# A two-layer decoder trunk: recurrence outputs normed four heads at a time, row norms taken per token, one block row's transfers on GpSimd

## The chip, the cores and the metric

The kernel runs on one core of a Trainium2 chip. The core has a matrix engine (PE, with its weight loads listed as PEld), a vector engine (DVE), a scalar engine with lookup tables (ACT), a general engine (POOL, also called GpSimd) and a queue engine (SP, also called SyncE). Each runs its own list of instructions in order; they meet at semaphores. DMA transfers are issued by SP and by POOL here. The metric is the time of one execution in microseconds (us).

## The reference, cut to what matters

Everything is float32, with 256 tokens of width 2048. Layer 0 mixes by two head groups side by side, spatial gating (A) and a gated linear recurrence (B), layer 1 by attention with a forget gate (C). Each is followed by a gated MLP with a short convolution. Every block starts with a row norm over the 2048 channels of a token.

```python
def rms_norm(x, gain):
    y = x * rsqrt(mean(x * x, axis=-1) + 1e-6); return y * gain

u, v, q, f, i, g = split(rms_norm(x) @ w_in)       # layer 0: six parts of 1024 columns
v = rms_norm(gelu(v) per head); y_a = gelu(u) * (causal(w_s) @ v + b)
k, decay = (1 - lb) * sigmoid(-f), lb + (1 - lb) * sigmoid(f)      # 8 heads of 128
o[t] = sum over s <= t of (q[t] . k[s], decayed from s to t) * i[s]
y_b = rms_norm(o per head) * silu(g)               # the norm that the change regroups
x = x + concat(y_a, y_b) @ w_out

q, k, v, g, f = split(rms_norm(x) @ w_c)           # layer 1: f has one column per head, 16
c = cumsum(log_sigmoid(f + b_f))                   # along the tokens
s = q @ k.T / sqrt(128) + c[t] - c[s]; y = softmax(causal s) @ v * sigmoid(g)
x = x + y @ w_out
```

The row factor rsqrt(mean(x*x)+eps) of a token is called R below. It multiplies a whole row, so the kernel may apply it to the products instead of to x. The norm of a recurrence head over its 128 channels has the same form; a factor R that multiplied q of token t multiplies all of o[t].

## The kernel before, in words

**Weights.** 820 pieces of 512 KB (some smaller) come from HBM through SP, into four buffers. `weights` (L179 to L183) issues the load; `halves` rounds the piece on ACT to the form that the profile calls fp32r (`wh`, L175) and subtracts on DVE what was lost (`wl`, L176). Each of the two has three buffers. The activations are split in the same way, and PE adds three products, high by high, high by low and low by high (L311 to L313 in `project_four`, L292 to L294 in `project_tok`, L266 and L269 in `project`). A weights piece feeds a dozen 128x512 matmuls in most projections.

**All other work goes between the pieces.** It is written as generators. `tick()` (L127) is called ahead of each weights piece and advances each generator in flight by one yield; `depth` says how many may be in flight and the rest wait in `queue`. `held(r)` and `tied(r)` order an instruction of a generator behind the newest weights operation or matmul, without a semaphore. Within these orders a scheduler at build time lists each engine's instructions by its own costs.

**Transposition of block rows.** `blocks` (L323) transposes 32x32 squares on DVE into `tmp`; `moves` (L327 to L333) sends 16 transfers of 32 KB to turn the squares' order, eight from SP and eight from GpSimd in alternation (L331).

**Layer 0, `mixer_ab` (L486).** The row norm of x sums squares into `acc` (128 channels-in-a-tile by 256 tokens). `Norm.finish` (L443 to L452) multiplies a matrix of ones by `acc` (L445), which gives the row sums along the free dimension on all 128 partitions, and makes R, 128x256; `finish_tok` (L430) makes the same factors with tokens on partitions, Rt, 128x2, from four small matmuls (L434). A matmul with a reversing matrix (L594) turns the second column of Rt upside down for the values of the recurrence (Rr).

The recurrence is a generator per head, `hgrn(h)` (L667 to L755). It takes three times a PSUM bank of the two of the pool `px`: `dg` for the diagonal (16 small matmuls, L681), `xps` for the levels (L714 to L721), `op` for the output (L743 to L745). The output of a head, 128 by 256, is squared and summed on ACT straight from the bank, once for each half of the tokens (L749), the factor is made (L751, a logarithm and an exponential on ACT), and two scaled copies take the output out of the bank to `o` (L753). For q, `fold` (L335 to L339) adds the two halves of the product and L802 and L803 multiply by R. `gated` (L768) multiplies the output by silu of the gate and sends the result through `blocks` and `moves`. Ahead of the projection the pieces of `w_g` and `w_u` go by, four heads each.

The output projection reads `w_abo` (L847 to L860), a quarter q of the output channels at a time. `add_four` (L460) evicts a quarter, transposes it with `blocks` and `moves` (all 16 at once for q = 0 and 3, in two lots for q = 1 and 2), and later adds it to x (L474) and feeds the next norm. The first four pieces of the second quarter are multiplied ahead of the last two of the first.

**Layer 1, `mixer_c` (L866).** `norm.finish()` (L888) makes R again, since the forget gate has tokens along the free dimension. `forget` (L896 to L902) multiplies the 16 gate columns by x in four 32-partition groups; `sums` (L904 to L929) adds the groups, multiplies by R (L919), takes log-sigmoid and the running sum (L926), and writes it to HBM (L928). `spread` (L931 to L934) reads it back to all partitions, four heads at a time, in 512 KB; `attend` adds it to the scores (L958).

The code that the profile's lines belong to:

Of the kernel before, what the change touches and what calls it, by code (L numbers as in the profile page):

```python
# [8 lines left out]
F32 = mybir.dt.float32  # L9
# [10 lines left out]
NH = 8  # L20
# [33 lines left out]
def tile_trunk(ctx: ExitStack, tc: tile.TileContext, x, pp_d, cst_d, mlev_d, msk_d,  # L54
# [12 lines left out]
    def nm(base):  # L67
        count[0] += 1
        return f"{base}_{count[0]}"
# [44 lines left out]
    def bank():  # L114
        return psum["pool"].tile([P, 512], F32, tag="px", name=nm("px"), bufs=psum["banks"])
# [211 lines left out]
    def moves(tmp, dst, queues=(nc.sync, nc.gpsimd), rows=range(4)):  # L327
        n = 2 * BLK
        for a in rows:
            for b in range(4):  # L330
                queues[(a + b) % len(queues)].dma_start(dst[BLK * b:BLK * (b + 1), :, a * n:(a + 1) * n],  # L331
                                  tmp[BLK * a:BLK * (a + 1), b * 4 * n:(b + 1) * 4 * n]
                                  .rearrange("p (m r) -> p m r", m=4))  # L333

    def fold(ps):  # L335
        t = tp.tile([P, S], F32, tag="ev", name=nm("ev"), bufs=3)
        SC.activation(t, ps[:, S:2 * S], AF.Copy)
        V.tensor_tensor(t, ps[:, 0:S], t, ALU.add)
        return t  # L339

    def project_norm(wsrc, acts, R, out=None, run=2):
        t = fold(project(wsrc, acts, run=run))
        if out is None:
            out = t
        V.tensor_tensor(out, t, R, ALU.mult)
        return out

    def split(dst, src, gain=None, eng=SC, turn=False):
        if turn:
            h, lo = (dst[:, i * S:(i + 1) * S].rearrange("p (t n) -> p t n", t=2) for i in range(2))  # L350
# [49 lines left out]
    class Norm:  # L400
# [39 lines left out]
            rsq(Rt, p2[:, 0:4].rearrange("p (t two) -> p t two", two=2)[:, :, 0], D)  # L440
            self.Rt = Rt

        def finish(self, tok=False):  # L443
            ps = bank()
            PE.matmul(ps[:, 0:S], ones, self.acc, start=True, stop=True)  # L445
            R = cp.tile([P, S], F32, tag="R", name=nm("R"), bufs=2)
            rsq(R, ps[:, 0:S], D)
            if not tok:
                return R
            for _ in self.finish_tok():  # L450
                pass
            return R, self.Rt  # L452
# [7 lines left out]
    def add_four(q, ps, z, tmp, dst, nxt, halves=1):  # L460
        for T in range(2):
            SC.activation(z[:, T], ps[T], AF.Copy)
        blocks(lambda T: z[:, T], tmp)
        moves(tmp, dst, rows=range(4 // halves))

        def rest():
            if halves == 2:
                yield
                moves(tmp, dst, rows=range(2, 4))
            for _ in range(LAG - 2 * (q == 3)):  # L470
                yield
            for i in range(4):
                m = 4 * q + i
                held(V.tensor_tensor(xT[m], xT[m], dst[:, i], ALU.add), "wl")  # L474
                nxt.feed(m)
                if q < 3 or i % 2:
                    yield
            if q == 3:
                for _ in range(WAIT):
                    yield  # L480
                yield from nxt.finish_tok()

        queue.append(rest())


    def mixer_ab(norm):  # L486
# [8 lines left out]
            return hp.tile([P, S], F32, tag="mg" if n == "mg" else "lf", name=nm(n), bufs=NH)  # L495


        gv, late = [], []

        def finish():  # L500
            for k in range(KT):
                norm.feed_square(k)
                if k % 2:
                    yield
            late.extend(norm.finish(tok=True))

        for g, ps in enumerate(project_first(w_v, norm, lambda: queue.append(finish()))):
            v = hp.tile([P, 2, 512], F32, tag="tok", name=nm("gv"), bufs=2)
            gv.append(v)
            if g == 0:  # L510
                SC.activation(v[:, 0], ps[0], AF.Copy)
                SC.activation(v[:, 1], ps[1], AF.Copy)
            else:
                drain()
                R, Rt = late
                last = ps
        A = norm.a

# [71 lines left out]
                yield  # L590


        ps = bank()
        PE.matmul(ps[:, 0:2], cst[:, K_REV:K_REV + P], Rt, start=True, stop=True)  # L594
        Rr = hp.tile([P, LANE], F32, tag="Rr", name="Rr")[:, 0:2]
        V.tensor_copy(Rr[:, 0:1], Rt[:, 0:1])
        V.tensor_copy(Rr[:, 1:2], ps[:, 1:2])


        gam = pp[:, C_GAM:C_GAM + 3 * NH]  # L600
# [6 lines left out]
        def bound():  # L607
# [9 lines left out]
            V.tensor_tensor(lb, e3[0], sm_, ALU.mult)  # L617
            V.tensor_scalar(lb, lb, 2.0 ** -63, None, ALU.max)

        queue.append(mixes())  # L620
        lf, kq = [], []

# [28 lines left out]
        depth[0] = 5  # L651

        itoks, left, os_ = [], [NH], []


        H = P // 2
# [10 lines left out]
        def hgrn(h):  # L667
# [75 lines left out]
            tied(PE.matmul(op[:, 0:P], st[:, 0], i0, start=True, stop=True))  # L743
            tied(PE.matmul(op[:, P:S], s128, i0, start=True, stop=False))
            tied(PE.matmul(op[:, P:S], s1, i1, start=False, stop=True))  # L745
            so = hp.tile([P, LANE], F32, tag="so", name=nm("so"), bufs=2)[:, 0:2]
            ot = hp.tile([P, P], F32, tag="ot", name=nm("ot"), bufs=1)
            for T in range(2):
                SC.activation(ot, op[:, T * P:(T + 1) * P], AF.Square,  # L749
                              accum_out=so[:, T:T + 1])  # L750
            rsq(so, so, P)  # L751
            for T in range(2):
                SC.activation(os_[h // 4][:, T, d0:d0 + P], op[:, T * P:(T + 1) * P], AF.Copy,  # L753
                              scale=so[:, T:T + 1])
            left[0] -= 1  # L755

        gz = []
# [36 lines left out]
        for h in range(NH):  # L794
            if h in (4, 7):
                values(len(itoks))
            while len(kq) <= h:
                tick()
            if h % 4 == 0:
                os_.append(hp.tile([P, 2, 512], F32, tag="o", name=nm("o"), bufs=2))  # L800
            z = fold(project(w_q[h], A))
            V.tensor_tensor(kq[h][:, 2], z[:, 0:P], R[:, 0:P], ALU.mult)  # L802
            V.tensor_tensor(back(kq[h][:, 1]), z[:, P:S], R[:, P:S], ALU.mult)  # L803
            queue.append(hgrn(h))
        for j in range(2):
            ps = project_four(w_g[4 * j:4 * j + 4], A, KT)
# [38 lines left out]
        for q in range(4):  # L845
            if q == 0:

                ps = stretch(0, (0, 2, 4, 6, 8, 10), more=True)
                ahead = stretch(1, (0, 2, 4, 6), more=True)
                stretch(0, (12, 14), ps=ps)  # L850
            elif q == 1:
                ps = stretch(1, (8, 10, 12, 14), ps=ahead)
            else:
                ps = stretch(q, range(0, KT, 2))
            z = hp.tile([P, 2, 512], F32, tag="tok", name=nm("zo"), bufs=2)
            tmp = hp.tile([P, 1024], F32, tag="E", name=nm("tmp"), bufs=2)
            dst = wide("dst").rearrange("p (m t) -> p m t", m=4)
            if q == 0:
                depth[0] = 2
            add_four(q, ps, z, tmp, dst, nxt, 2 if q in (1, 2) else 1)  # L860
        es.close()
        banks(ctx, 4)
        return nxt
# [2 lines left out]
    def mixer_c(norm):  # L866
# [18 lines left out]
        early.append(project_tok(w_cqkv[CH // 4], norm))  # L885
        drain()
        depth[0] = 2
        R, Rt = norm.finish(), norm.Rt  # L888
        yB = []
        gq = hp.tile([P, LANE], F32, tag="gq", name="gq")[:, 0:1]  # L890
        V.tensor_scalar(gq, pp[:, C_QN:C_QN + 1], float(P) ** -0.5, None, ALU.mult)
# [4 lines left out]
        def forget():  # L896

            ps = pm.tile([P, 512], F32, tag="pm", name=nm("pm"))
            for k in range(KT):
                r = k % 4 * BLK  # L900
                PE.matmul(ps[r:r + CH, 0:S], w2[:, k], xT[k], start=k < 4, stop=k >= KT - 4, skip_group_check=True)
            return ps  # L902

        def sums(ps, fc):  # L904
            yield
            yield
            f, fa, on = (hp.tile([CH, S], F32, tag=n, name=n) for n in ("f", "fa", "on"))
            c = hp.tile([P, 512], F32, tag="f2", name="f2")[0:CH].rearrange("p (g n) -> p g n", g=2)
            for g, t in ((1, c[:, 0]), (2, c[:, 1]), (3, f)):
                r = SC.activation(t, ps[BLK * g:BLK * g + CH, 0:S], AF.Copy)  # L910
                if g == 1:
                    held(r)
            yield
            held(V.tensor_tensor(f, ps[0:CH, 0:S], f, ALU.add), "wl")
            for g in range(2):
                V.tensor_tensor(f, f, c[:, g], ALU.add)
            V.memset(fc, 0.0)
            V.memset(on, 1.0)
            V.tensor_tensor(f, f, R[0:CH], ALU.mult)  # L919
            V.tensor_scalar(f, f, pp[0:CH, C_BF:C_BF + 1], None, ALU.add)  # L920
            yield
            held(SC.activation(fa, f, AF.Abs))
            act(fa, fa, AF.Exp, scale=-1.0)
            act(fa, fa, AF.Ln, bias=one1[0:CH])
            V.scalar_tensor_tensor(f, f, 0.0, fa, ALU.min, ALU.subtract)
            V.tensor_tensor_scan(fc[0:CH], on, f, 0.0, ALU.mult, ALU.add)  # L926
# [73 lines left out]
        for g in range(CH // 4):  # L1000
            qkv = []
            ss = hp.tile([P, 2, 2, LANE // 4], F32, tag="ss", name=nm("ss"), bufs=2)[..., 0:4]
            for j in range(3):
                if g == 0 and j == 2:
                    fc, cd = hp.tile([P, S], F32, tag="fc", name="fc"), []
                    queue.append(sums(forget(), fc))
# [294 lines left out]
```

## Time and profile before

| | |
|---|---|
| runs | 2288.38, 2287.43 and 2288.41 us, median 2288.38 |
| span of the profiled execution | 2287.3 us (the page gives no other time for it) |
| instructions | 32261, of them 10832 matmuls |
| granted PE clock | full in all 40 slices |
| HBM read | 435.24 MB; DMA mean 210 GB/s |
| busy | PE 2280.8, DVE 1559.8, ACT 1309.6, POOL 361.2 us |

The profile is one execution; its span is 1.1 us below the median of the three runs. In a row of the timeline the columns are start, duration, engine, line, operation, output and inputs, sizes and count; a bracket at the end gives the engine's idle time before it and what ended it. Matmuls overlap, so the distance of two starts tells more than a duration. A group row gives busy time and mean nanoseconds of one, then the idle time before the group.

### The profile page before, as it was taken

The numbers are of one execution on the slowest core, as the hardware profiler recorded it, in microseconds if no ns is written. First come the engines' busy times: TensorE is split into PE (matmuls) and PEld (weight loads), VectorE is DVE, ScalarE is ACT, GpSimd is POOL, SyncE is SP. The second block draws the span as 40 slices with busy tenths as digits, with TensorE's granted clock in tenths as the row PEclk, the third lists the DMA queues.
The fourth block names the chain that finished last, engine by engine and source line by source line (L and its number), as shares of the span: only waits on it lengthen the run. The fifth ranks groups of instructions, "written<-read, shape, count | busy, mean of one in ns | idle before, by whom it ended". The sixth has DMA issues, their size and how long they took to land.

```text
span 2287.3 us, 32261 instructions
## 1 busy us (share of the span) xinstructions
PE 2280.8 (100%) x10832; PEld 1893.5 (83%) x10832; DVE 1559.8 (68%) x2309; ACT 1309.6 (57%) x1980; POOL 361.2 (16%) x662
## 2 busy tenths in 40 slices
PE   9999999999999999999999999999999999999999
PEld 8888888888888888888888888888888888888887
DVE  7788767777467656766875675767776476657766
ACT  7677756666456445654565555655665465456642
POOL 0121221212012002111111111211211012012102
PEclk9999999999999999999999999999999999999999
DMA  8655767778667667776666655777777677667765
GB/s 288 195 169 160 215 199 235 238 216 234 193 208 221 206 201 213 220 213 186 213 227 203 194 177 181 220 224 242 225 217 218 195 216 210 209 205 216 223 204 174
DMA packets 489415, 480.45 MB, mean 210 GB/s; under 512 B 114112, under 2 KB 457168, under 8 KB 489120
## 3 DMA queue, kind: packets, MB, share of 16 engines
q1 hardware_dynamic: 467040, 453.54, 64.2%
q0 software_dynamic: 20480, 22.50, 4.3%
q10 hardware_dynamic: 1728, 2.35, 0.3%
q8 instruction: 85, 1.39, 0.3%
q14 instruction: 82, 0.67, 0.1%
HBM read 435.24 MB, written 2.11 MB: 191 GB/s over the span
## 4 chain that ended last, share of the span: by engine, by line
PE 97%; DVE 2%; ACT 1%; issue 0%; SPq 0%; DMA 0%; DVEq 0%; ACTq 0%
PE pm L311 26%; PE pm L312 26%; PE pm L313 26%; PE pm L292 4%; PE pm L294 4%; PE pm L293 4%; PE pm L193 1%; PE pm L266 1%; PE pm L217 1%; DVE wl L176 0%; PE pm L269 0%; ACT wh L175 0%; DVE kq L701 0%; PE px L955 0%; SPq L331 0%
## 5 line engine op out<-in xcount | busy, mean ns | idle before, releaser
L176 DVE TENSOR_TENSOR wl<-w,wh 128x1024 fp32r<-128x1024 f32 (+1 forms) x820 | 996.9, 1219 | 637.0 <-ACT wh L175 629.3
L175 ACT ACTIVATE wh<-w 128x1024 fp32r<-128x1024 f32 (+1 forms) x820 | 862.5, 1054 | 786.0 <-PE pm L313 552.3
L311 PE MATMUL pm<-wh,a 128*128 128x512 f32 x1728 | 674.4, 390 | 0.0
L312 PE MATMUL pm<-wl,a 128*128 128x512 f32 x1728 | 672.5, 389 | 0.0
L313 PE MATMUL pm<-wh,a 128*128 128x512 f32 x1728 | 672.5, 389 | 0.0
L331 POOL DMA_DIRECT2D zt<-tmp x413 | 223.5, 549 | 1201.6 <-DVE tmp L324 1089.8
L313 PEld LDWEIGHTS pm<-wh,a 128*128 128x128 f32 x1728 | 324.4, 188 | 67.4
L312 PEld LDWEIGHTS pm<-wl,a 128*128 128x128 f32 x1728 | 324.4, 188 | 67.3 <-DVE wl L176 0.5
L311 PEld LDWEIGHTS pm<-wh,a 128*128 128x128 f32 x1728 | 324.4, 188 | 67.1
L311 PE MATMUL pm<-wh,hid 128*128 128x512 f32 x688 | 267.6, 389 | 0.0
L312 PE MATMUL pm<-wl,hid 128*128 128x512 f32 x688 | 267.6, 389 | 0.0
L313 PE MATMUL pm<-wh,hid 128*128 128x512 f32 x688 | 267.6, 389 | 0.0
L331 POOL DMA_DIRECT2D turn<-tmp x160 | 86.7, 550 | 504.5 <-DVE tmp L324 256.7
L292 PE MATMUL pm<-wh,a 128*128 128x512 f32 x416 | 165.2, 397 | 0.0
L294 PE MATMUL pm<-wh,a 128*128 128x512 f32 x416 | 162.1, 390 | 0.0
L293 PE MATMUL pm<-wl,a 128*128 128x512 f32 x416 | 162.0, 389 | 0.0
L311 PEld LDWEIGHTS pm<-wh,hid 128*128 128x128 f32 x688 | 129.2, 188 | 26.9
L313 PEld LDWEIGHTS pm<-wh,hid 128*128 128x128 f32 x688 | 129.2, 188 | 26.8
L312 PEld LDWEIGHTS pm<-wl,hid 128*128 128x128 f32 x688 | 129.2, 188 | 26.7
L1105 ACT ACTIVATE conv<-zt,pp 128x256 f32<-128x256 f32 x176 | 95.9, 589 | 26.1 <-DMA zt<-tmp 22.2
L324 DVE STREAM_TRANSPOSE tmp<-z 128x512 f32<-128x512 f32 x120 | 83.4, 704 | 18.9 <-ACT z L1091 18.4
L294 PEld LDWEIGHTS pm<-wh,a 128*128 128x128 f32 x416 | 78.1, 188 | 16.6
(244 smaller groups left out, 2075.6 us busy)
## 6 DMA issues: line engine op xcount, KB each, us to landing
w<-in_w_up SPq DMA_DIRECT2D x352, 512.0 KB, 4.4
w<-in_w_dn SPq DMA_DIRECT2D x176, 512.0 KB, 4.5
w<-in_w_cqkv SPq DMA_DIRECT2D x96, 512.0 KB, 4.3
w<-in_w_abo SPq DMA_DIRECT2D x32, 512.0 KB, 4.6
w<-in_w_cg SPq DMA_DIRECT2D x32, 512.0 KB, 4.3
w<-in_w_co SPq DMA_DIRECT2D x32, 512.0 KB, 4.3
zt<-tmp SPq DMA_DIRECT2D x414, 32.0 KB, 2.7
zt<-tmp POOLq DMA_DIRECT2D x413, 32.0 KB, 2.5
```

Of the source, the lines that this page charges most:

```text
L175: r = deep["wh"] = SC.activation(wh, w, AF.Copy)
L176: deep["wl"] = V.tensor_tensor(wl, w, wh.bitcast(F32), ALU.subtract)
L193: PE.matmul(ps[g][T], a[:, o + T * P:o + (T + 1) * P], t[:, i * 512:(i + 1) * 512], start=k + i + j == 0, stop=k + i == KT - 1 and j == 2)
L292: PE.matmul(ps[T], ah, h, start=k + i == 0, stop=False)
L293: PE.matmul(ps[T], ah, l, start=False, stop=False)
L294: deep["last"] = PE.matmul(ps[T], al, h, start=False, stop=k + i == KT - 1)
L311: PE.matmul(ps[T], ah, h, start=not begun and k + i == ks[0], stop=False)
L312: PE.matmul(ps[T], ah, l, start=False, stop=False)
L313: deep["mm"] = deep["last"] = PE.matmul(ps[T], al, h, start=False, stop=not more and k + i == ks[-1] + 1)
L324: V.transpose(tmp.rearrange("p (b m i t) -> p b m i t", b=4, m=4, t=2)[:, :, :, :, T], src(T).rearrange("p (m b j) -> p b m j", m=4, b=4))
L331: queues[(a + b) % len(queues)].dma_start(dst[BLK * b:BLK * (b + 1), :, a * n:(a + 1) * n], tmp[BLK * a:BLK * (a + 1), b * 4 * n:(b + 1) * ...
L1105: held(SC.activation(c, z, AF.Identity, bias=pp[:, cb:cb + 1], scale=w(2)))
```

## The change

1. **Recurrence.** A head's output leaves its bank by one 128x256 copy on ACT, unscaled. The squares are taken from the copy in SBUF, with R of the token (Rt) as the scale, into one column per head. After every fourth head, one yield later, one factor computation on 128x8 serves four heads, is multiplied by Rt, and two 128x512 multiplies on DVE (held behind a subtraction of weights) apply it.
2. **q without R.** The two halves of q's product are added straight from PSUM into their places, two 128x128 adds; `fold`, `project_norm` and the 128x256 R of layer 0 are gone with their matmul (L445) and factor computation.
3. **Mirror.** The reversed column of Rt is made on DVE by a generator in `queue` (a broadcast copy, a small copy, a transpose, a transpose of the reversed view, four 32x1 copies) instead of by the matmul L594.
4. **Quarter 0's transfers.** All 16 transfers of `moves` for q = 0 are issued by GpSimd.
5. **Layer 1's R.** Four matmuls of 32 columns of ones by 64 tokens of `acc` each put the row sums into the four 32-partition groups of one bank; the factor is made on 128x64, and four 16x64 copies on ACT lay it out as 16x256 for the gate. The L445 matmul and the 128x256 factor computation of `mixer_c` are gone. Factor and copies are made in `sums`, behind its first two yields, where before R was made ahead of `forget`.

```diff
-    def fold(ps): ...
-    def project_norm(wsrc, acts, R, out=None, run=2): ...
-        def finish(self, tok=False):
-            ps = bank()
-            PE.matmul(ps[:, 0:S], ones, self.acc, start=True, stop=True)
-            R = cp.tile([P, S], F32, tag="R", name=nm("R"), bufs=2)
-            rsq(R, ps[:, 0:S], D)
...
-        moves(tmp, dst, rows=range(4 // halves))
+        moves(tmp, dst, queues, rows=range(4 // halves))
...
-            late.extend(norm.finish(tok=True))
+            for _ in norm.finish_tok():
+                pass
...
-        ps = bank()
-        PE.matmul(ps[:, 0:2], cst[:, K_REV:K_REV + P], Rt, start=True, stop=True)
-        V.tensor_copy(Rr[:, 0:1], Rt[:, 0:1])
-        V.tensor_copy(Rr[:, 1:2], ps[:, 1:2])
+        def mirror():
+            yield
+            held(V.tensor_copy(ra, Rt[:, 1:2].to_broadcast([P, BLK])), "wl")
+            V.tensor_copy(Rr[:, 0:1], Rt[:, 0:1])
+            V.transpose(rb, ra)
+            V.transpose(ra, view(rb, BLK - 1, (-1, BLK)))
+            for a in range(4):
+                V.tensor_copy(Rr[BLK * (3 - a):BLK * (4 - a), 1:2], ra[BLK * a:BLK * (a + 1), 0:1])
...
+        queue.append(mirror())
         queue.append(mixes())
...
-            so = hp.tile([P, LANE], F32, tag="so", name=nm("so"), bufs=2)[:, 0:2]
+            o = os_[h // 4]
+            SC.activation(o[:, :, d0:d0 + P], op[:, 0:S].rearrange("p (t d) -> p t d", t=2), AF.Copy)
+            so = sos[:, h // 4]
             for T in range(2):
-                SC.activation(ot, op[:, T * P:(T + 1) * P], AF.Square,
-                              accum_out=so[:, T:T + 1])
-            rsq(so, so, P)
-            for T in range(2):
-                SC.activation(os_[h // 4][:, T, d0:d0 + P], op[:, T * P:(T + 1) * P], AF.Copy,
-                              scale=so[:, T:T + 1])
+                SC.activation(ot, o[:, T, d0:d0 + P], AF.Square, scale=Rt[:, T:T + 1],
+                              accum_out=so[:, T, h % 4:h % 4 + 1])
+            if h % 4 == 3:
+                yield
+                rsq(so, so, P)
+                V.tensor_tensor(so, so, Rt.unsqueeze(2).to_broadcast([P, 2, 4]), ALU.mult)
+                for T in range(2):
+                    o4 = o[:, T].rearrange("p (h d) -> p h d", d=P)
+                    held(V.tensor_tensor(o4, o4, so[:, T].unsqueeze(2).to_broadcast([P, 4, P]), ALU.mult), "wl")
...
-            z = fold(project(w_q[h], A))
-            V.tensor_tensor(kq[h][:, 2], z[:, 0:P], R[:, 0:P], ALU.mult)
-            V.tensor_tensor(back(kq[h][:, 1]), z[:, P:S], R[:, P:S], ALU.mult)
+            ps = project(w_q[h], A)
+            z = tp.tile([P, S], F32, tag="ev", name=nm("ev"), bufs=3)
+            SC.activation(z, ps[:, S:2 * S], AF.Copy)
+            V.tensor_tensor(kq[h][:, 2], ps[:, 0:P], z[:, 0:P], ALU.add)
+            V.tensor_tensor(back(kq[h][:, 1]), ps[:, P:S], z[:, P:S], ALU.add)
...
-            add_four(q, ps, z, tmp, dst, nxt, 2 if q in (1, 2) else 1)
+            add_four(q, ps, z, tmp, dst, nxt, 2 if q in (1, 2) else 1, (nc.sync, nc.gpsimd) if q else (nc.gpsimd,))
...
-        R, Rt = norm.finish(), norm.Rt
+        Rt = norm.Rt
...
+            pr = bank()
+            for g in range(4):
+                PE.matmul(pr[BLK * g:BLK * (g + 1), 0:LANE], ones[:, 0:BLK], norm.acc[:, LANE * g:LANE * (g + 1)],
+                          start=True, stop=True)
...
+            Rq = hp.tile([P, LANE], F32, tag="Rq", name="Rq")
+            R = hp.tile([CH, S], F32, tag="Rf", name="Rf")
+            rsq(Rq, pr[:, 0:LANE], D)
+            for g in range(4):
+                SC.activation(R[:, LANE * g:LANE * (g + 1)], Rq[BLK * g:BLK * g + CH], AF.Copy)
...
-            V.tensor_tensor(f, f, R[0:CH], ALU.mult)
+            V.tensor_tensor(f, f, R, ALU.mult)
```

More of the change, by code (lines that the diff above doesn't have):

```diff
@@ L333, in moves @@
                                   .rearrange("p (m r) -> p m r", m=4))
[L335 to L346, printed above, removed]
     def split(dst, src, gain=None, eng=SC, turn=False):
@@ L441, in finish_tok @@
             self.Rt = Rt
-        def finish(self, tok=False):
-            ps = bank()
-            PE.matmul(ps[:, 0:S], ones, self.acc, start=True, stop=True)
-            R = cp.tile([P, S], F32, tag="R", name=nm("R"), bufs=2)
-            rsq(R, ps[:, 0:S], D)
[L448 to L452, printed above, removed]
     def add_x(m, ps):
@@ L458, in add_x, with add_four @@
         V.tensor_tensor(xT[m], xT[m], t, ALU.add)
-    def add_four(q, ps, z, tmp, dst, nxt, halves=1):
+    def add_four(q, ps, z, tmp, dst, nxt, halves=1, queues=(nc.sync, nc.gpsimd)):
         for T in range(2):
@@ L495, in keep @@
             return hp.tile([P, S], F32, tag="mg" if n == "mg" else "lf", name=nm(n), bufs=NH)
-        gv, late = [], []
+        gv = []
         def finish():
@@ L514, in mixer_ab @@
                 drain()
-                R, Rt = late
+                Rt = norm.Rt
                 last = ps
@@ L590, in mixes @@
                 yield
-        ps = bank()
-        PE.matmul(ps[:, 0:2], cst[:, K_REV:K_REV + P], Rt, start=True, stop=True)
         Rr = hp.tile([P, LANE], F32, tag="Rr", name="Rr")[:, 0:2]
-        V.tensor_copy(Rr[:, 0:1], Rt[:, 0:1])
-        V.tensor_copy(Rr[:, 1:2], ps[:, 1:2])
+        ra, rb = (hp.tile([P, LANE], F32, tag=n, name=n)[:, 0:BLK] for n in ("ra", "rb"))
+        def mirror():
[6 more added lines that the diff above has]
+                V.tensor_copy(Rr[BLK * (3 - a):BLK * (4 - a), 1:2], ra[BLK * a:BLK * (a + 1), 0:1])
         gam = pp[:, C_GAM:C_GAM + 3 * NH]
@@ L653, in mixer_ab @@
         itoks, left, os_ = [], [NH], []
+        sos = hp.tile([P, LANE], F32, tag="so", name="sos")[:, 0:2 * NH].rearrange("p (j t h) -> p j t h", j=2, t=2)
         H = P // 2
@@ L887, in mixer_c @@
         depth[0] = 2
-        R, Rt = norm.finish(), norm.Rt
+        Rt = norm.Rt
         yB = []
@@ L901, in forget, with sums @@
                 PE.matmul(ps[r:r + CH, 0:S], w2[:, k], xT[k], start=k < 4, stop=k >= KT - 4, skip_group_check=True)
-            return ps
-        def sums(ps, fc):
+            return ps, pr
+        def sums(ps, pr, fc):
             yield
             yield
+            Rq = hp.tile([P, LANE], F32, tag="Rq", name="Rq")
[3 more added lines that the diff above has]
+                SC.activation(R[:, LANE * g:LANE * (g + 1)], Rq[BLK * g:BLK * g + CH], AF.Copy)
             f, fa, on = (hp.tile([CH, S], F32, tag=n, name=n) for n in ("f", "fa", "on"))
@@ L1005, in mixer_c @@
                     fc, cd = hp.tile([P, S], F32, tag="fc", name="fc"), []
-                    queue.append(sums(forget(), fc))
+                    queue.append(sums(*forget(), fc))
                 if g and j == 2:
```

## The prediction

> **What bounds the kernel now.** The page's head comes first.
>
> ```profile
> span 2287.3 us, 32261 instructions
> ...
> PE 2280.8 (100%) x10832; PEld 1893.5 (83%) x10832; DVE 1559.8 (68%) x2309; ACT 1309.6 (57%) x1980; POOL 361.2 (16%) x662
> ```
>
> PE is busy for 2280.8 of 2287.3 us, so 6.5 us are idle in the whole execution. An edit gains only if it removes matmuls or one of PE's rare waits. The list of what PE waited for says which waits there are; its columns are us, times and the longest. The first rows that concern the change are these two:
>
> ```profile
> PE px L681 <- ACT o L753: 1.1, 1, 1.1
> ...
> PE pm L312 <- DVE wl L176: 0.6, 1, 0.6
> ```
>
> One matmul of the recurrence waits for the copies that leave its PSUM bank, and one product waits for a subtracted weights piece. DVE and ACT work released elsewhere is worth nothing by itself, since DVE has 727 us idle (2287.3 less 1559.8) and ACT 978. That is why this sum goes by four places on PE, and why it is small.
>
> **A. The bank of the recurrence (edit 1).** Matmul starts tell lost time better than idle time, since matmuls overlap. The PE timeline around three heads:
>
> ```profile
> 158.22 0.33 PE L721 MATMUL px<-E 128*32 128x64 f32 x7
> 158.63 0.43 PE L681 MATMUL px<-kq 128*32 128x64 f32 x16
> ...
> 171.58 0.33 PE L721 MATMUL px<-E 128*32 128x64 f32 x7
> 171.70 0.43 PE L681 MATMUL px<-kq 128*32 128x64 f32 x16
> 172.07 0.50 PE L292 MATMUL pm<-wh,a 128*128 128x512 f32 x1
> ...
> 184.56 0.33 PE L721 MATMUL px<-E 128*32 128x64 f32 x7
> 185.99 0.43 PE L681 MATMUL px<-kq 128*32 128x64 f32 x16 [1.10 <-ACT o L753]
> ```
>
> Undisturbed, L681 starts 0.12 after the L721 group (171.58 to 171.70). At 158 the distance is 0.41 and at 184 it is 1.43: lost are 0.29 and 1.31, together 1.60 us. What held the bank at 184, in ACT's timeline:
>
> ```profile
> 181.72 0.28 ACT L749 ACTIVATE ot<-px 128x128 f32<-128x128 f32 x1
> ...
> 185.31 0.62 ACT L753 ACTIVATE o<-px,so 128x128 f32<-128x128 f32 x2
> ```
>
> The output was there at 181.72, when the first square read it. Then came the factor and, in ACT's list, a weights rounding, so the scaled copies ended only at 185.93, and L681 started at 185.99. After the change the raw copy stands where the square stood. The two 128x128 copies took 0.62; one of 128x256 takes at most that, so the bank is free by 181.72 + 0.62 = 182.34, 2.3 us ahead of 184.68, when PE would want it. The gain lies between 0 (the copy placed behind a rounding again) and 1.60. I take 1.60: the comparison of the two instruction orders has the copy of each head ahead of its squares, and squares and factor no longer hold the bank.
>
> **B. A late weights piece (edit 4).** SP's, DVE's and PE's timelines:
>
> ```profile
> 331.58 1.64 SPq L181 DMA_DIRECT2D w<-in_w_abo  x3
> 337.24 6.47 SPq L331 DMA_DIRECT2D dst<-tmp  x8
> 343.81 8.29 SPq L181 DMA_DIRECT2D w<-in_w_abo  x6
> ```
>
> ```profile
> 334.25 1.23 DVE L176 TENSOR_TENSOR wl<-w,wh 128x1024 fp32r<-128x1024 f32 x1 [1.49 <-ACT wh L175]
> ...
> 349.00 1.22 DVE L176 TENSOR_TENSOR wl<-w,wh 128x1024 fp32r<-128x1024 f32 x1 [2.78 <-ACT wh L175]
> ```
>
> ```profile
> 346.78 0.39 PE L312 MATMUL pm<-wl,ya 128*128 128x512 f32 x1
> 347.01 0.39 PE L313 MATMUL pm<-wh,ya 128*128 128x512 f32 x1
> ...
> 349.27 0.39 PE L311 MATMUL pm<-wh,ya 128*128 128x512 f32 x1
> 350.28 0.50 PE L312 MATMUL pm<-wl,ya 128*128 128x512 f32 x1 [0.62 <-DVE wl L176]
> ```
>
> Eight transfers of quarter 1 stand in SP's queue from 337.24; they waited for their transposition. The weights piece behind them is issued only at 343.81, its subtraction starts at 349.00, and the product that needs it starts 1.01 after the one before it, where 0.23 is the pitch (346.78 to 347.01): 0.78 us lost. In the changed order quarter 0's eight transfers are gone from SP, and four pieces instead of three stand ahead of quarter 1's. The fourth takes the buffer that the subtraction of 334.25 frees at 335.48, 8.3 us earlier than 343.81 and before 337.24, so it holds nothing up. The gain is between 0 (another piece becomes late) and 0.78. The next subtraction would be wanted 0.78 earlier, and its load goes forward too, into the place at 343.81. I take 0.78.
>
> **C and D. Matmuls removed and added (edits 2, 3 and 5).** PE's timeline at the three removed matmuls:
>
> ```profile
> 49.44 0.59 PE L445 MATMUL px<-acc,ones 128*128 128x256 f32 x2
> 49.87 0.50 PE L434 MATMUL px<-ones,acc 128*128 128x2 f32 x4
> ...
> 53.52 0.28 PE L594 MATMUL px<-Rt,cst 128*128 128x2 f32 x2
> 53.66 0.48 PE L313 MATMUL pm<-wh,a 128*128 128x512 f32 x1
> ...
> 1142.80 0.59 PE L445 MATMUL px<-acc,ones 128*128 128x256 f32 x2
> 1143.32 1.92 PE L901 MATMUL pm<-x,w 128*16 128x256 f32 x32
> ```
>
> C, layer 0: 0.43 (49.44 to 49.87) and 0.14 (53.52 to 53.66), 0.57 in all. D, layer 1: 0.52 goes (1142.80 to 1143.32) and four matmuls of 32 rows by 64 columns come, eight passes. The nearest row is L681, of the same size: 16 passes in 0.37 (171.70 to 172.07), so eight cost 0.18 and D gains 0.34. The dearest near row is L434, four passes in 0.50, which would make 1.0 and lose 0.48; were the passes hidden in what surrounds them, D would gain 0.52. I take 0.34, by form and size.
>
> **What is costed at nothing.** DVE: eight 128x256 adds go for q, four 128x512 multiplies and eight small operations of the mirror come. ACT: fewer factors, one copy per head instead of two. All of it lies in the idle time of both; the place where that cover is thinnest is the first rival. Quarter 0 now waits for 16 issues on GpSimd instead of eight; that is the third. The gate row of layer 1 is made later; that is the second.
>
> **Sum.** 1.60 + 0.78 + 0.57 + 0.34 = 3.29, against the profiled execution's 2287.3: 2284.0. The median of the runs is 1.1 above this span (2288.38), so the runs should give 2285.1; I say 2285.2. With D at its best the ceiling is 3.47.
>
> **Rival 1, the grouped norm stands in front of a weights piece.** After the eighth head, at the third piece of w_u, DVE and PE show:
>
> ```profile
> 251.46 0.69 DVE L778 TENSOR_TENSOR gz<-gz,o 128x512 f32<-128x512 f32 x1 [2.49 <-ACT gz L98]
> ...
> 252.89 1.18 DVE L176 TENSOR_TENSOR wl<-w,wh 128x1024 fp32r<-128x1024 f32 x1
> ```
>
> ```profile
> 254.23 0.41 PE L312 MATMUL pm<-wl,a 128*128 128x512 f32 x1
> ```
>
> The subtraction ends at 254.07 and is used at 254.23: 0.16 to spare. The change puts two multiplies like L778 (0.69 each, 1.38) ahead of L778 on DVE. They fall into its 2.49 of idle time if the factor is ready in time, and then cost nothing; against the rival speaks also that two scaled copies leave ACT there. If none were covered, the piece would be 1.38 - 0.16 = 1.2 late: 2285.2 + 1.2 = 2286.4. Chance 0.13.
>
> **Rival 2, the gate row of layer 1 comes late.** DVE and POOL in layer 1, and the landing times of cb:
>
> ```profile
> 1154.73 0.68 DVE L926 TENSOR_TENSOR_SCAN fc<-on,f 16x256 f32<-16x256 f32 x1
> ...
> 1170.89 0.35 DVE L958 SCALAR_TENSOR_TENSOR sc<-px,ct,cb 128x128 f32<-128x128 f32 x1 [0.63 <-PE px L955]
> ```
>
> ```profile
> 1158.44 2.18 POOL L934 DMA_DIRECT2D cb<-cd  x4 [1.46 <-DMA cd<-fc]
> ```
>
> ```profile
> DMA to landing us min/median/max: 9.1/11.1/14.1
> ```
>
> The four copies and the multiply by R now come in `sums`, interleaved with more pieces of weights. Following the changed order along ACT and DVE I estimate cb's issue 3.5 us later, at 1161.9, by one and a half pieces of 12 products at 0.23. The first of the four must be there for L958 at 1170.89. Landing in 9.1 it comes at 1171.0, on time; in 11.1 at 1173.0 it is 2.1 late, in 14.1 at 1176.0 it is 5.1 late. Heads go on PE in turn, and a delay of L958 reaches PE almost whole. Price 2.1 to 5.1, on the estimate 2287.3 to 2290.3. I hold 9.1 for the first of four as likelier, since the later ones queue behind it. Chance 0.14.
>
> **Rival 3, slower: GpSimd issues too slowly.** Quarter 0's 16 transfers go one after the other from its queue:
>
> ```profile
> 326.63 4.33 POOL L331 DMA_DIRECT2D dst<-tmp  x8 [27.95 <-DVE tmp L324]
> ```
>
> ```profile
> L331 POOL DMA_DIRECT2D dst<-tmp x32: 548/548/551, 326.6 to 386.0; - x32
> L474 DVE TENSOR_TENSOR x<-x,dst x16: 381/418/424, 336.0 to 394.0; 128x256 f32<-128x256 f32 x16
> ...
> DMA to landing us min/median/max: 1.8/2.2/4.2
> ```
>
> At 0.548 each the last lands at 326.63 + 16 x 0.548 + 2.2 = 337.6. What it may delay: in the changed order three adds to x (0.42 each) stand ahead of the subtraction that the product of 346.78 needs. With 1.23 for the subtraction the transfers must be there by 346.78 - 1.23 - 1.26 = 344.3, so up to 0.97 us per issue they are harmless. The loss passes the gain of 3.3 and 0.2% more (4.6 us, about what a measurement of this kernel can tell from no change) from 7.9 us late, or 1.46 per issue. If every issue waited out one subtraction (0.55 + 1.23 = 1.78), the last would land at 357.3, 13.0 late: 2298. Against it stands the row itself: 32 such issues took 548 to 551 ns, some of them beside subtractions.
>
> [...]
>
> Rival 3 keeps 0.12, since in this trace GpSimd never sends 16 of them in one run.
>
> **How the numbers follow.** The sum holds with 0.57, rivals 1 to 3 with 0.13, 0.14 and 0.12, and 0.04 is left for a gain that no row shows, beyond 4.6 us. Within 0.2% lie the sum and, up to 2290.3, rivals 1 and 2: 0.57 + 0.13 + 0.14 = 0.84. Slower is rival 3, 0.12; faster 0.04. The range begins at 2284.0, the fastest run shown (2287.43) less the ceiling of 3.47, and reaches into rival 2 up to 2289.6, leaving out rival 3, the top of rival 2 and the gain unseen, some 0.2.
>
> **What would show it.** A: no wait of L681 for an ACT copy, and 0.12 from L721 to each L681. B: four weights loads ahead of quarter 1's transfers on SP, and 0.23 between products there. C, D: the matmuls gone, and the four new ones within 0.2 of L901's start. Rival 1: PE waiting for `wl` near 254. Rival 2: PE idle behind L958, with cb landing last. Rival 3: the 16 issues longer than 0.55, or adds to x that wait for `dst`. The prediction is wrong if PE's idle time grows at a place that none of these names, since the orders of all engines were made anew.

## The result, and the profile after

The changed kernel takes 2293.55 us in the median of seven runs (2290.97 to 2298.2), the kernel before beside it 2287.59. The ratio is 1.0026, 95% interval 1.0017 to 1.0035: 0.26% slower, where 2285.2 was forecast in a range of 2284.0 to 2289.6. A run's time is 1.9 us more than its span (2293.55 against 2291.7 in the profiled execution); the text on record took 1.1, since it had no time for the execution before.

The page's head of the changed kernel, and its list of what PE waited for:

```profile
span 2291.7 us, 32213 instructions
...
PE 2282.2 (100%) x10834; PEld 1892.8 (83%) x10834; DVE 1555.9 (68%) x2285; ACT 1307.6 (57%) x1962; POOL 361.9 (16%) x670
```

```profile
PE pm L292 <- ACT wh L175: 1.4, 1, 1.4
PE pm L312 <- DVE wl L176: 1.3, 2, 0.7
PE warm L144 <- DVE ones L84: 1.1, 1, 1.1
PE pm L293 <- DVE wl L176: 0.8, 1, 0.8
PE px L978 <- ACT sc L98: 0.6, 2, 0.4
```

L681's wait for the copies is gone, and so is the one in quarter 1. New waits have come, all those above 0.3 behind 1150 us (the start apart), and only that of L978 at a place that the forecast named. Where the time went shows when the first use of each of the 800 weights pieces in the main projections is set side by side in two traces. Up to 360 us the changed kernel gets ahead by 3.2 us of the profiled execution before, and by 0.3 more at L901. Then it falls behind in steps: 0.43 at 489, 1.04 at 1175, 1.58 and 2.74 at 1239 and 1245, 0.91 at 1636, 1.03 at 1963. These make 7.7.

The largest place, PE's timeline in layer 1:

```profile
1237.12 0.39 PE L294 MATMUL pm<-wh,a 128*128 128x512 f32 x1
1238.93 0.51 PE L292 MATMUL pm<-wh,a 128*128 128x512 f32 x1 [1.42 <-ACT wh L175]
1240.19 0.54 PE L293 MATMUL pm<-wl,a 128*128 128x512 f32 x1 [0.76 <-DVE wl L176]
1240.53 0.63 PE L294 MATMUL pm<-wh,a 128*128 128x512 f32 x1
1240.96 0.63 PE L292 MATMUL pm<-wh,a 128*128 128x512 f32 x1
1241.38 0.63 PE L293 MATMUL pm<-wl,a 128*128 128x512 f32 x1
```

PE starts 1.81 and 1.26 after the matmul before, where 0.23 is the pitch, so 2.6 us are lost. After that the matmuls start 0.43 apart instead of 0.23 until 1243.9: the clock is lowered to a half for 3.41 us, and another 1.7 go. The windows around this place, with the granted clock in the third column from the end, first of the changed kernel, then of the kernel before:

```profile
1237.00:1246.00 9.00, 6.82 (x25) 5.04 (x24) 4.34 (x6) 6.33 (x9) 0.00 (x0) 0.81 0.51 162
```

```profile
1236.00:1245.00 9.00, 9.00 (x43) 7.58 (x42) 5.70 (x10) 5.89 (x8) 0.00 (x0) 1.00 0.81 275
```

The granted clock was 0.81 in this stretch and 1.00 before the change. What came late is in the timelines of GpSimd (POOL), SP and ACT of the changed kernel:

```profile
1224.15 0.55 POOL L331 DMA_DIRECT2D turn<-tmp  x1 [18.69 <-DVE tmp L324]
1227.22 3.80 POOL L331 DMA_DIRECT2D turn<-tmp  x7 [2.52 <-issue]
```

```profile
1223.88 5.11 SPq L331 DMA_DIRECT2D turn<-tmp  x8
1229.09 2.97 SPq L181 DMA_DIRECT2D w<-in_w_cqkv  x4
```

```profile
1230.35 0.94 ACT L950 ACTIVATE qk<-turn,gq 128x256 f32<-128x256 f32 x2
1237.00 0.93 ACT L950 ACTIVATE qk<-turn,pp 128x256 f32<-128x256 f32 x2 [5.71 <-DMA w<-in_w_cqkv]
1237.84 1.99 ACT L175 ACTIVATE wh<-w 128x1024 fp32r<-128x1024 f32 x2
```

GpSimd sends one transfer and then nothing for 2.52 us, with no wait that the profile shows. Its last three transfers of this group therefore leave after SP has issued weights at 1229.09. The last leaves at 1230.47 and lands 6.2 us later, at about 1236.7, where the median of the group is 1.9. ACT's copy at 1237.00 needs it: the row names a load of weights, which landed at nearly the same time, but L950 reads `turn`. Two weights roundings stand behind that copy in ACT's list, and PE behind those. The kernel before has the same group without the pause, and the pause elsewhere:

```profile
1226.20 4.33 POOL L331 DMA_DIRECT2D turn<-tmp  x8 [18.70 <-DVE tmp L324]
...
1275.48 0.55 POOL L331 DMA_DIRECT2D turn<-tmp  x1 [44.96 <-ACT wh L175]
1278.56 3.78 POOL L331 DMA_DIRECT2D turn<-tmp  x7 [2.52 <-issue]
```

Counted along GpSimd's queue, pauses of 2.2 to 2.5 us stand in both traces behind the transfers numbered 113, 219, 326, 432 and 538. The change gives this queue eight more transfers in layer 0 (634 instead of 626), so every pause falls on a piece of work eight transfers earlier. That was the theory to test. The rivals were the late gate row and the changed work of layer 0.

### The profile page after: what moved, and what is told of

Its sections match the earlier page's. It is cut to its first block, busy times and chain, and to the rows that moved or that the text cites. A ratio compares the mean times of both kernels' runs of the same rounds, so it can differ in the third digit from the quotient of the medians.

```text
span 2291.7 us, 32213 instructions
## 1 busy us (share of the span) xinstructions
PE 2282.2 (100%) x10834; PEld 1892.8 (83%) x10834; DVE 1555.9 (68%) x2285; ACT 1307.6 (57%) x1962; POOL 361.9 (16%) x670
## 3 DMA queue, kind: packets, MB, share of 16 engines
q0 software_dynamic: 20736, 22.77, 4.4%
HBM read 435.24 MB, written 2.11 MB: 191 GB/s over the span
## 5 line engine op out<-in xcount | busy, mean ns | idle before, releaser
L311 PEld LDWEIGHTS pm<-wh,a 128*128 128x128 f32 x1728 | 324.4, 188 | 67.4
L313 PEld LDWEIGHTS pm<-wh,a 128*128 128x128 f32 x1728 | 324.4, 188 | 67.4
L1107 DVE SCALAR_TENSOR_TENSOR conv<-zt,pp,conv 128x255 f32<-128x255 f32 x176 | 78.1, 478 | 24.9 <-ACT conv L1106 16.5
```

Source lines behind the costliest of these rows:

```text
L311: PE.matmul(ps[T], ah, h, start=not begun and k + i == ks[0], stop=False)
L313: deep["mm"] = deep["last"] = PE.matmul(ps[T], al, h, start=False, stop=not more and k + i == ks[-1] + 1)
L1107: V.scalar_tensor_tensor(c[:, 1:], z[:, :S - 1], w(1), c[:, 1:], ALU.mult, ALU.add)
```

## The experiments

The runs of before on the same chip had medians of 2287.03, 2287.03 and 2287.06. Medians are quoted below; the intervals of the ratios are about 0.1% on either side.

**Edit 4 undone.**

```diff
-add_four(q, ps, z, tmp, dst, nxt, 2 if q in (1, 2) else 1, (nc.sync, nc.gpsimd) if q else (nc.gpsimd,))
+add_four(q, ps, z, tmp, dst, nxt, 2 if q in (1, 2) else 1)
```

> The changed kernel with edit 4 undone: quarter 0's transfers go half from SP and half from GpSimd again, so GpSimd sends 626 transfers as before instead of 634. Theory, the queue's stall: in both traces GpSimd pauses 2.2 to 2.5 us ahead of its transfers numbered 113, 219, 326, 432 and 538, and eight more transfers move these pauses to other work; undone, they return to where they were, and with the gains of the recurrence bank (1.6), the row norm matmuls (0.9) and layer 1's (0.3), less the late gate row (1.0), the time is 2287.6 - 2.8 + 1.0 = 2285.8. Rival, the grouped norm, the mirror or the late gate row cost the 6 us: it stays at 2292 to 2294, since only quarter 0 moves back.

Measured: 2286.67 (2285.72 to 2287.27), ratio 0.9997, interval 0.9987 to 1.0006. Edit 4 undone takes 6.9 us off the changed kernel. The pauses are back at 489.5, 904.0, 1273.3, 1609.7 and 2023.8, and the wait list of PE has one row of 0.3 beside the start. None of the losses at 489, 1239, 1636 and 1963 is in its trace, nor the one at 1175. The gain forecast, 1.8 (2287.6 to 2285.8), came as 0.4.

**Edit 4 alone, on the kernel before.** The same line and the `queues` argument, nothing else.

> The kernel before with edit 4 alone: all 16 transfers of quarter 0 on GpSimd. Theory, the queue's stall: the four losses seen in the changed kernel behind shifted pauses (0.4, 4.3, 0.9 and 1.0, together 6.7) come, and the late weights piece on SP (0.8) goes: 2287.6 + 6.7 - 0.8 = 2293.5. Rival, other edits cost it: 2287.6 - 0.8 = 2286.8.

Measured: 2290.64 (2288.93 to 2295.07), ratio 1.0016, interval 1.0006 to 1.0025. The direction is the theory's, the size some 0.6 of it: 3.6 us, where 5.9 was forecast (2287.6 to 2293.5). Its profiled execution, the slowest of the ten at 2295.07, has the pause at 1225.4, and behind it two starts on PE come 2.11 and 1.26 after the one before.

**Eight small blank transfers on the kernel before.** They stand at the head of GpSimd's queue; the instruction lists of the other engines are unchanged.

```diff
+blank = sd.tile([8, P], F32, tag="blank", name="blank")      # in HBM
+for i in range(8):
+    nc.gpsimd.dma_start(blank[i:i + 1], ones[i:i + 1, :])
```

> The kernel before with eight transfers of 512 bytes added at the head of GpSimd's queue, which bring nothing; all other engines keep their lists. Theory, the queue's stall counted in transfers: the pauses fall eight transfers earlier in the rest of the queue, as in the changed kernel, 2287.6 + 5 to 7 = 2293 to 2295, and the third pause stands in front of the second transfer of the group at 1226. Rival, counted in bytes or in descriptors: eight such transfers shift it by almost nothing, 2287.6. Rival, the loss comes from the changed work: 2287.6.

Measured: 2287.38 (2286.05 to 2288.36), ratio 1.0000. Here the theory's unit was wrong, not its rule: the pauses stand behind transfers 119, 225, 332, 438 and 544, so the eight blanks, of 512 bytes each, counted together as two transfers. The time is that of the rivals (2287.6 was forecast), not the theory's 2293 to 2295. In the group at 1224 the pause stands ahead of the eighth transfer:

```profile
1223.90 3.79 POOL L331 DMA_DIRECT2D turn<-tmp  x7 [18.71 <-DVE tmp L324]
1229.81 0.55 POOL L331 DMA_DIRECT2D turn<-tmp  x1 [2.12 <-DMA turn<-tmp]
```

One late transfer cost a distance of 1.26 between two starts on PE at 1237, and no lowered clock. Neither transfers nor bytes alone are counted, nor pieces alone: the eight blanks are 4 KB in eight rows, as the kernel writes them, and the two transfers they count for 64 KB in 256 pieces.

**Edit 4 kept, eight other transfers moved to SP.** The first gated output's transfers of layer 0 all go from SP.

```diff
-moves(tmp, t.rearrange("p (m t) -> p m t", m=4))
+moves(tmp, t.rearrange("p (m t) -> p m t", m=4), (nc.sync,) if j == 0 else (nc.sync, nc.gpsimd))
```

> The changed kernel with the eight GpSimd transfers of the first gated output (layer 0, four heads) sent from SP instead, ahead of quarter 0: 626 on GpSimd again with edit 4 kept. Theory, the queue's stall: all pauses stand where they stood before, the gains stay: 2287.6 - 3.5 + 1.0 = 2285.1, plus at most 1 if SP's weights loads come late behind the eight. Rival, anything else in the change costs it: 2292 to 2294.

Measured: 2287.46 (2286.11 to 2288.7), ratio 1.0001. Quarter 0 on one queue does no harm once the pauses stand at 489.7, 904.2, 1273.5, 1609.7 and 2024.0. The 2.4 us above the forecast are partly SP's: 16 transfers in 11.4 us delay the weights behind them, and between 241 and 261 PE falls 1.6 behind the changed kernel.

**The kernel before once more.**

> The kernel before once more, unchanged, for a second profiled execution. Theory, part of the sum stood on waits of one execution: the profiled one spans 2287.3 us, and a run's time is 1.9 us more than its span in the later runs, so it took about 2289.2, the slow end of before's 2286.2 to 2289.0. The waits of 1.3 at 184 (recurrence bank) and of 0.8 at 350 (late weights piece) are then smaller or absent, and the span is near 2285. Rival, they belong to the kernel: both return, span near 2287.

Measured: span 2284.8, time 2286.6. Of the two waits that carried the sum, the one at 350 is absent and the one at 184 was 0.3 instead of 1.1:

```profile
PE warm L144 <- DVE ones L84: 1.1, 1, 1.1
PE px L681 <- ACT o L753: 0.3, 1, 0.3
```

The execution that the forecast was read from was 2.5 us longer than this one, and 1.9 of that are these two places and the one at 158. By this execution the gains of the recurrence bank and of SP's order are 0.46 and 0.1.

**Eight full blank transfers on the kernel before.** As above, with 128 pieces each:

```diff
+nc.gpsimd.dma_start(blank[BLK * i:BLK * (i + 1)].rearrange("p (a b) -> p a b", a=4)[..., 0:BLK],
+                    ones[BLK * (i % 4):BLK * (i % 4 + 1)].rearrange("p (a b) -> p a b", a=4))
```

> The kernel before with eight transfers added at the head of GpSimd's queue that have as many pieces as those of moves (128 each), and bring nothing; all other engines keep their lists. The 512-byte ones counted as a quarter transfer each. Theory, the queue's pause: these count as one each, the pauses stand where the changed kernel has them (after transfers 113, 219, 326, 432, 538, the third behind the first transfer of the group at 1225), and the time is 2287.0 + 4 to 6.7 = 2291 to 2294. Rival, all of quarter 0 on one queue does the harm, not the place of the pauses: 2287 to 2287.5.

Measured: 2290.41 (2287.99 to 2292.24), ratio 1.0014, interval 1.0005 to 1.0024. Eight transfers that bring nothing, at the head of the queue, make the kernel before 3.4 us slower, nearly what edit 4 costs, and 0.6 less than the least that was forecast (2291). The pauses are behind transfers 113, 219, 326, 432 and 538 of the longer queue, and the place is the same:

```profile
1224.12 0.55 POOL L331 DMA_DIRECT2D turn<-tmp  x1 [18.71 <-DVE tmp L324]
1227.20 3.79 POOL L331 DMA_DIRECT2D turn<-tmp  x7 [2.53 <-issue]
```

Starts on PE are 2.06 and 1.26 apart there and 1.14 at 1957, in this execution without a lowered clock. Against the second execution of before these are the only places where its trace loses more than 0.3 at once.

**One full blank transfer on the changed kernel.**

> The changed kernel with one such transfer added at the head of GpSimd's queue: the third pause then stands between two groups, ahead of the first transfer at 1224. Theory, the pause runs as soon as the transfer ahead of it is issued: it lies in the 19 us in which GpSimd has nothing to send, the loss of 4.3 goes, and the time is 2287 to 2289.5, the other three losses left. Rival, it runs when the next transfer is to be issued: all eight come 2.5 later and the time stays at 2291 to 2294.

Measured: 2293.23 (2289.97 to 2296.01), ratio 1.0027, interval 1.0016 to 1.0038. The rival holds. The pause is not taken in the idle 19 us before: the whole group leaves late, and the copy waits as long.

```profile
1227.71 4.33 POOL L331 DMA_DIRECT2D turn<-tmp  x8 [21.30 <-DVE wl L176]
```

```profile
1238.24 0.93 ACT L955 ACTIVATE qk<-turn,pp 128x256 f32<-128x256 f32 x2 [5.98 <-DMA w<-in_w_cqkv]
```

SP's first transfer of the group left at 1224.84, GpSimd's at 1227.71.

**Edits 1 to 3 alone.** Edit 4 undone as above, and `mixer_c` and `Norm.finish` as before the change:

```diff
-        Rt = norm.Rt
+        R, Rt = norm.finish(), norm.Rt
...
-            V.tensor_tensor(f, f, R, ALU.mult)
+            V.tensor_tensor(f, f, R[0:CH], ALU.mult)
```

> The changed kernel with edits 4 and 5 undone: edits 1 to 3 alone (recurrence, q, mirror). Theory: layer 1's matmul comes back (0.3 dearer than the run without edit 4 at 2286.7), and the gate row is there 4.3 earlier, which saves at most 1.0 where it was late: 2286.0 to 2287.0. Rival, the late gate row costs the 1.0 in most executions: 2285.9 or less.

Measured: 2286.14 (2285.68 to 2286.87), ratio 0.9996, interval 0.9986 to 1.0006. It is the shortest median of all, and every one of its ten runs lies below the median of before, 2287.03; the ratio's interval does not exclude 1. It lies in the range that the theory gave. PE waits for nothing but its start:

```profile
PE warm L144 <- DVE ones L84: 1.1, 1, 1.1
```

With edit 5 on top the median is 0.5 more (2286.67). That edit 5 costs this is not shown: the two traces put 0.31 to its credit at the gate and nothing against it at 1175, and what the longer one loses lies at the start (0.5) and at 348 (0.6), far ahead of the gate.

**Edit 5 undone in the changed kernel.** Edits 1 to 4, by the same diff, with edit 4 kept.

> The changed kernel with edit 5 alone undone: edits 1 to 4, the gate row early as before. The eight added blanks (2290.4) and edit 4 alone (2290.6) cost 3.4 and 3.6, the whole change 6 above before, so some 2.5 to 3 are left that the pauses alone do not make. Theory: they come from the late gate row, whose wait (1.0 in the changed kernel, 2.5 in the run with one blank) adds to the pauses: 2290.6 less the 0.9 that edits 1 to 3 bring = 2289.5 to 2290.5. Rival: they come from edits 1 to 3 with the shifted pauses, or from the lowered clock alone: 2292 to 2294.

Measured: 2289.87 (2288.04 to 2291.88), ratio 1.0012, interval 1.0002 to 1.0021. The forecast of the theory holds: most of what the pauses alone do not make goes with edit 5. In medians, edits 1 to 3 save 0.9 (2287.03 to 2286.14), edit 4 costs 3.7 on top (to 2289.87), and edit 5 another 3.7 on top of that (to 2293.55; 3.2 if each is taken against its own runs of before, 2287.06 and 2287.59). The intervals of the two ratios just overlap, and so do the runs: the shortest of the changed kernel is 2290.97, the longest here 2291.88.

The wait at 1237 is far shorter here than in the changed kernel (1.42), with the same pause and the same place of it:

```profile
1235.02 0.94 ACT L952 ACTIVATE qk<-turn,pp 128x256 f32<-128x256 f32 x2 [4.49 <-DMA turn<-tmp]
```

```profile
1236.96 0.49 PE L292 MATMUL pm<-wh,a 128*128 128x512 f32 x1 [0.21 <-ACT wh L175]
1238.22 0.50 PE L293 MATMUL pm<-wl,a 128*128 128x512 f32 x1 [0.77 <-DVE wl L176]
```

Set side by side, the changed kernel's trace loses to this one 1.0 at 1175, behind the late gate row, 1.2 by the longer wait at 1237, and some 1.6 by the clock lowered after it. That makes the 3.6 between the spans (2291.7 and 2288.1), with small steps both ways. The clock goes with the runs, too: five of the seven of the changed kernel have a mean clock below 1.000, one of the ten here. Only the first of the three is tied to edit 5 by a row. Whether edit 5 also lengthens the wait at 1237 stays open, since the waits there are as long (1.67 and 1.72) in the runs with eight full blanks and with edit 4 alone, whose gate rows are early.

## Why the prediction was wrong

**The step that failed** is the one on what is costed at nothing: "Quarter 0 now waits for 16 issues on GpSimd instead of eight; that is the third." It priced the moved transfers by the work that waits for them. They also count in GpSimd's queue for all that comes later, 900 us on: put at nothing, this cost 3.6 us by edit 4 alone (2290.64 against 2287.03), and eight transfers that bring nothing cost 3.4. The late gate row, put at nothing beside it, is the second failed term (rival 2 below). The rows were there to be read: the kernel before shows five pauses such as [2.52 <-issue] inside groups of eight transfers, at nearly equal distances in count. The forecast quoted the issue times of quarter 0 only and never asked what the queue's other idle rows were.

**Rival 3** named the right edit, the right queue and the wrong mechanism. Issue times in quarter 0 stayed at 551 ns, as in all 40 issues to `dst`; the last of its 16 left in time, and the three adds to x ran at 338.55 without a wait. Its place and its price, 1.78 per issue behind a subtraction, did not occur. The pauses come by the count of what was sent, not by what VectorE was doing: in the two kernels they stand behind the same numbers, at times 11 to 84 us apart.

**A, the recurrence bank: right in mechanism, mis-sized.** The raw copy leaves the bank before the weights rounding, and L666 follows 0.12 behind its group, as these rows of the changed kernel show (its L666 and L706 are L681 and L721 of before):

```profile
179.58 0.39 ACT L732 ACTIVATE o<-px 128x256 f32<-128x256 f32 x1
```

```profile
183.46 0.33 PE L706 MATMUL px<-E 128*32 128x64 f32 x7
183.58 0.44 PE L666 MATMUL px<-kq 128*32 128x64 f32 x16
```

Against the first execution 1.6 us come back, as forecast. Against the second it is 0.46, all of it at 184.

**B, the late piece: right in mechanism, mis-sized.** Four pieces do stand ahead of quarter 1's transfers, and the product of 350.28 gains the 0.78 that was forecast, on that execution alone. In the second execution of before the wait is absent, and the gain is 0.1.

```profile
325.54 8.04 SPq L181 DMA_DIRECT2D w<-in_w_abo  x4
334.96 5.72 SPq L331 DMA_DIRECT2D dst<-tmp  x8
```

Both terms, 2.38 of the sum of 3.29, were waits of one execution taken for the kernel's. By the 1.9 us between span and time that execution took about 2289.2, longer than all seven runs of before beside the result (2287.15 to 2288.41); the text on record did not have the 1.9.

**C and D: right.** Layer 1's eight passes start 0.14 before the gate's matmuls, and the step at that place is 0.31 where 0.34 was forecast. L594's step is 0.23 (0.14 forecast). L445's is 0.43, as forecast, against both executions of before.

```profile
1140.08 0.32 PE L893 MATMUL px<-acc,ones 128*32 128x64 f32 x8
1140.22 1.91 PE L897 MATMUL pm<-x,w 128*16 128x256 f32 x32
```

**Rival 1 did not occur.** The two multiplies of the eighth head lie in DVE's idle time, as the forecast had it, and the subtraction of the third piece of w_u follows in time:

```profile
247.42 1.29 DVE L744 TENSOR_TENSOR o<-o,sos 128x512 f32<-128x512 f32 x2 [0.23 <-DVE sos L741]
...
250.60 1.18 DVE L176 TENSOR_TENSOR wl<-w,wh 128x1024 fp32r<-128x1024 f32 x1
```

**Rival 2 occurred, at half its lower price in the trace.** cb is issued at 1162.70 (1161.9 estimated), and L959, which is L958 of before, waits for it. That the issue is so near is in part luck: one and a half pieces of 12 products at 0.23 make 4.1, not the 3.5 of the estimate, and most of the 4.3 it moved is that GpSimd waited 5.11 for the row to land in HBM, instead of 1.46.

```profile
1162.70 2.19 POOL L935 DMA_DIRECT2D cb<-cd  x4 [5.11 <-DMA cd<-fc]
```

```profile
1170.10 0.35 DVE L959 SCALAR_TENSOR_TENSOR sc<-px,ct,cb 128x128 f32<-128x128 f32 x1 [3.05 <-DMA cb<-cd]
```

PE is 1.0 late behind it, 2.5 in the run with one full blank, and not late in the two runs where the pauses had been put back, with cb issued just as late there (1162.74 and 1162.47).

## What to carry to other kernels

Eight transfers moved to another queue put all five of its pauses eight transfers earlier here, from 467 to 1943 us: if a queue pauses at regular counts, find them in the trace before, and ask on which group they will fall after the move. A wait in one profiled execution is worth its time only if a second execution shows it again; the profile's span against the spread of the runs tells whether it was a slow one. In an engine that works in order, look at what stands behind a copy that waits for transfers; here two weights roundings did (ACT, 1237.84, 1.99 us).

## What the runs showed of the hardware

GpSimd's queue paused for 2.2 to 2.5 us behind its transfers 113, 219, 326, 432 and 538, that is after 106 or 107 at a time, in the kernel before and in the changed one; nearly all of these transfers have 128 pieces. Eight transfers of 512 bytes counted together as two (the first pause behind 119), and a pause there lasted 2.12. In the run with one full blank the pause was taken when the next transfer was to go out, not before, though the queue had been idle for 19 us: the group left 2.87 behind SP's first transfer (1227.71 against 1224.84), where the changed kernel's first left 0.27 behind it. What is counted stays open: not transfers, bytes or pieces alone, and not the packets of the profile's page, of which both runs with eight blanks have 256 more on this queue than the kernel before (20736 against 20480). Why the queue pauses, no run shows.

PE's clock was lowered after idle times of 1.42 and 0.76 us with one matmul between them, for some eight matmuls at 0.43 instead of 0.23. About the same idle times (1.67 and 0.76) left it at full speed in the run with eight full blanks:

```profile
1239.16 0.50 PE L292 MATMUL pm<-wh,a 128*128 128x512 f32 x1 [1.67 <-ACT wh L175]
1240.42 0.50 PE L293 MATMUL pm<-wl,a 128*128 128x512 f32 x1 [0.76 <-DVE wl L176]
1240.76 0.39 PE L294 MATMUL pm<-wh,a 128*128 128x512 f32 x1
1240.98 0.39 PE L292 MATMUL pm<-wh,a 128*128 128x512 f32 x1
```

The traces record the granted clock with its times, and these times tell the cases apart. The clock was halved for 3.41 us in the changed kernel (1240.49 to 1243.91) and with one full blank (1242.31 to 1245.72; mean clock 0.999 in both), and for twice that, 6.83 us, with edit 4 alone (1240.57 to 1247.39; mean 0.998). Counted in steps of the recorded 3.413 us from the moment when the clock first rose, each of these starts falls on a step. In the changed kernel it is 362 steps from the rise at 4.87, and its next drop, at 2291.80 behind PE's last work, comes at 670; in the kernel before the rise is at 6.97 and the only drop, at its end, 668 steps later. In the step just ahead of the lowered clock PE was idle for 2.18 us (changed kernel), 2.04 (one full blank) and 1.87 (edit 4 alone). In the run with eight full blanks (mean clock 1.000) the boundary between two steps, 1238.62, falls into the idle time, which is split into 1.13 and 1.30; the clock stayed up. In the traces of before and of the changed kernel no other step between the rise and the last work of PE has more than 1.10 us of idle time (before, at 184.46) or 0.62 (changed, at 2284.98), and none of them was followed by a lowered clock. (With edit 4 alone the clock stayed low for a second step, although PE was idle for only 0.61 us of the first.)

Where the boundary falls differs from one execution to the next, the clock having first risen at 4.87 us in the changed kernel's and 6.97 in that of before, and so does the loss of 1.7 or more. By an estimate this makes most of the spread of the changed kernel's runs, 7.2 us where the 31 of before beside the first experiments spread over 2.9: the longest, 2298.2, has a mean clock of 0.997, by which 7 us are lost (0.003 of 2296.4, give or take 1 by rounding), and the shortest, 2290.97, has 1.000.
